# The sums of weight blocks in two squared-ReLU MLPs, moved from GpSimd to VectorE

## The chip, the core and the metric

The kernel runs on one core of a Trainium2 chip. The metric is the device time of one execution in microseconds. A core has a matrix engine (TensorE, "PE" in the profile, with its weight loads as "PEld"), VectorE ("DVE"), ScalarE ("ACT"), GpSimd ("POOL"), and SyncE ("SP"), which here only issues transfers. POOL issues transfers too, among them those that add to what lies in DRAM.

## The reference, cut to what matters

Two layers of a residual network over 1024 tokens of width 1024. Each layer mixes tokens (a recurrent block in layer 0, a forgetting attention in layer 1, each beside a memory cross-attention) and then applies an MLP of width 4096:

```python
def sqrelu_mlp(h, w1, w2):
    return jnp.square(jax.nn.relu(h @ w1)) @ w2

def reference(x, mem, ...):
    for layer in range(DEPTH):          # DEPTH = 2
        ...                             # token mixer, memory attention
        x = x + jnp.concatenate([y_mix, y_mem], axis=-1) @ w_out[layer]
        x = x + sqrelu_mlp(rms_norm(x, norm_mlp[layer]), w_mlp_in[layer], w_mlp_out[layer])
    return x
```

All tensors are float32.

## The kernel before, in words

**Precision.** TensorE multiplies in fp32r, a rounded form of float32. Every operand is therefore split into a high part, written by ScalarE as a rounding copy, and a low part, the operand less its high part, written by VectorE. A product then takes three matmuls: high times high, high times low, low times high (`t3`). For weights the two halves of a split are `_wpart`: the copy at line 316 (tile `wh`), the difference at line 317 (tile `wl`). For activations they are lines 474 and 477 (`split_sb`; both write a tile `r`) or 468 and 469 (`split`).

**Seven products in place of eight.** The MLPs use a scheme of Strassen's kind. Both factors are cut in two by two blocks, and seven products of block sums replace the eight block products. One *unit* (class `Unit`) is one two-by-two set of weight blocks a11, a12, a21, a22, each 128 x 1024, of which the seven left factors are formed: a11, a12, S2, S3, S1, a22 and S4, in this order. Each of the two MLPs runs over eight groups g, and each group over two units: a `w1` unit (`mlp_z`, the hidden layer) and a `w2` unit (`mlp_out`, the output layer). That makes 32 units, and seven products of 24 matmuls for each.

**Block sums.** `_wunit` makes a factor. For six of the seven it only splits a buffer. For S2 it also forms the sums, in place, in two halves of 512 columns: a11 - a21 (line 355, becomes S3), x = a22 - S3 (line 356, is S2 and lies in a float32 tile `f`), a12 - x (line 357, becomes S4); then over all 1024 columns a21 + a22 (line 360, becomes S1). So a unit has seven summing instructions: six of 128 x 512 and one of 128 x 1024. The engine is `G`: VectorE where `unit.dve` is true, GpSimd elsewhere. `plan_mlp` sets it for the `w1` unit of group 0 alone, once for each layer. The splits of S2, at line 317 from the tile `f`, are on ScalarE and VectorE in either case.

**Weights on their way.** Raw blocks come from DRAM by SP into four buffers `wr` (line 312). A buffer takes its next block when its last factor has been split. The split factors lie in a ring of three pairs `wh`, `wl`, so a factor is split at most two products ahead of the one that uses it (`wnext`, `_wsplit`).

**Activations.** `mlp_z` ends a hidden block by an addition from PSUM (line 1033), a rectification and scaling (line 1037), a square on ScalarE (line 1038) and block sums of its own (lines 1138, 1141, 1147, 1149), and then splits for the right factors of `mlp_out`. ScalarE copies first partial results out of PSUM at line 1028. In all groups but the last, `mlp_out` sends results by adding transfers from the POOL queue (line 1172, tile `xspill`), and a tile is free again when its transfer has landed. In the last group, GpSimd adds some results (line 1192) or fetches with adding transfers (line 1195). In layer 1 the first products of groups 0 to 3 are made earlier ("parked"), so the units of these groups hold fewer factors, but the sums are all there.

**Order.** The Python code emits instructions in program order. The tile framework, with `schedule_with_timeline_sim=True`, then fixes each engine's order at build time with a planner that plays the program through with costs of its own, and takes, of what is ready, what was emitted first. On the chip each engine works its own queue strictly in that order.

Of the kernel before, what the change touches and what calls it, by code (L numbers as in the profile page):

```python
# [175 lines left out]
class Builder:  # L176
# [825 lines left out]
    def plan_mlp(self, l, parked, wait):  # L1002
        for g in wait:
            self.plan_unit("w1", 8 * l + g, Unit.ALL[1:2])
        for g in range(8):
            u = self.plan_unit("w1", 8 * l + g, Unit.ALL[2:] if g in parked + wait else Unit.ALL)
            u.dve = g == 0
            self.plan_unit("w2", 8 * l + g)

    def product(self, banks, parts, start, done=None):  # L1010
        w = self.wnext()
# [779 lines left out]
```

## Time and profile before

| | |
|---|---|
| runs of the kernel before | 2135.48, 2134.29, 2131.20 us; median 2134.29 us |
| the profiled execution | 2132.37 us, span 2130.7 us |
| PE busy | 2071.5 us, 97% of the span |
| DVE busy | 1663.3 us, 78% |
| ACT busy | 1141.9 us, 54% |
| POOL busy | 864.0 us, 41% |
| adding transfers on POOL (line 1172) | 224, 284.7 us busy |
| mean granted TensorE clock | 0.988 of full speed |

The first MLP takes the stretch from some 340 to 980 us, the second from some 1505 us to the end, with a few of its first products a little earlier. A row of the groups reads: line, engine, operation, output <- input, shapes, count, then busy time in us and the mean of one in ns, then the time that the engine stood idle just before them and what ended it. A row of the timeline reads: start and length in us, engine, line, operation, and in brackets the idle time before it with the engine, tile and line that ended it.

### The profile page before, as it was taken

How to read it: one execution, taken by the hardware profiler on the slowest of the kernel's cores; microseconds unless marked ns; L12 is line 12 of the kernel's file. 1: busy time of each engine (PE TensorE's matmuls, PEld its weight loads, DVE VectorE, ACT ScalarE, POOL GpSimd, SP SyncE). 2: the span in 40 equal slices, each digit the busy share in tenths (PEclk: the TensorE clock that was granted, in tenths of full speed). 3: DMA queues.
4: the chain of work that ended last, by engine and by line, in shares of the span. 5: the costliest groups of instructions: out<-in, count | busy, mean ns of one | idle time of the engine just before them, and what ended most of it. 6: DMA issues, size and time to landing. Idle time of an engine off the chain costs nothing. (4 is left out here: it accounts for less than half of the span.)

```text
span 2130.7 us, 30055 instructions
## 1 busy us (share of the span) xinstructions
PE 2071.5 (97%) x10466; PEld 1727.4 (81%) x10466; DVE 1663.3 (78%) x2708; ACT 1141.9 (54%) x2160; POOL 864.0 (41%) x844
## 2 busy tenths in 40 slices
PE   9999999999999999988999999999999999999998
PEld 8898878878778778767998998777777877787786
DVE  7988698877877877887677778776787768868777
ACT  6755655544454454555555646566544554445443
POOL 2222321535535525545342333422054645445444
PEclk8999999999999999989999999999999999999999
DMA  5422452546545635627768446934546675364474
GB/s 180 140 77 93 135 184 94 101 89 128 101 97 119 111 87 119 156 86 199 276 218 290 133 138 214 299 122 129 161 99 139 138 150 101 85 140 94 89 173 119
DMA packets 126392, 298.44 MB, mean 140 GB/s; under 512 B 14176, under 2 KB 16288, under 8 KB 126240
## 3 DMA queue, kind: packets, MB, share of 16 engines
q1 hardware_dynamic: 82464, 208.36, 29.4%
q0 software_dynamic: 43776, 88.17, 23.2%
q8 instruction: 82, 1.34, 0.3%
q14 instruction: 70, 0.57, 0.1%
HBM read 187.32 MB, written 109.15 MB: 139 GB/s over the span
## 5 line engine op out<-in xcount | busy, mean ns | idle before, releaser
L317 DVE TENSOR_TENSOR wl<-wr,wh 128x1024 fp32r<-128x1024 f32 (+2 forms) x362 | 441.2, 1229 | 108.5 <-ACT wh L316 104.1
L1017 PE MATMUL pspt<-r,wh 128*128 128x512 f32 x1536 | 485.1, 396 | 7.2 <-DVE r L477 2.6
L1172 POOL DMA_DIRECT2D xspill<-f x224 | 284.7, 1963 | 287.5 <-DVE f L1033 284.1
L316 ACT ACTIVATE wh<-wr 128x1024 fp32r<-128x1024 f32 (+3 forms) x411 | 306.0, 766 | 141.4 <-PE pss L1017 41.2
L1017 PEld LDWEIGHTS pspt<-r,wh 128*128 128x128 f32 x1536 | 289.0, 188 | 77.9 <-DVE r L477 4.3
L1017 PE MATMUL pss<-r,wh 128*128 128x512 f32 x1024 | 329.6, 400 | 19.8 <-ACT f L1028 8.1
L477 DVE TENSOR_TENSOR r<-f,r 128x512 fp32r<-128x512 f32 x282 | 230.1, 826 | 98.5 <-ACT r L474 39.9
L1017 PE MATMUL pspt<-r,wl 128*128 128x512 f32 x768 | 305.6, 398 | 0.2
L1017 PE MATMUL pspj<-r,wh 128*128 128x512 f32 x832 | 265.8, 399 | 2.1 <-DVE f L1033 1.0
L1017 PEld LDWEIGHTS pss<-r,wh 128*128 128x128 f32 x1024 | 192.6, 189 | 75.9 <-DVE r L477 13.9
L385 PE MATMUL pspj<-wh,r 128*128 128x256 f32 (+1 forms) x1280 | 248.5, 286 | 2.3 <-DVE r L1322 0.8
L474 ACT ACTIVATE r<-f 128x512 fp32r<-128x512 f32 x282 | 173.5, 626 | 106.2 <-DMA xspill<-f 49.0
L1038 ACT ACTIVATE f<-f 128x512 f32<-128x512 f32 x128 | 80.9, 632 | 269.5 <-DVE f L1037 269.4
L385 PEld LDWEIGHTS pspj<-wh,r 128*128 128x128 f32 x1280 | 201.6, 188 | 5.3 <-DVE r L1322 1.0
L1017 PE MATMUL pss<-r,wl 128*128 128x512 f32 x512 | 203.6, 398 | 0.0
L355 POOL TENSOR_TENSOR wr<-wr,wr 128x512 f32<-128x512 f32 x60 | 95.7, 1778 | 249.0 <-DVE wl L317 233.2
L1017 PEld LDWEIGHTS pspj<-r,wh 128*128 128x128 f32 x832 | 156.3, 189 | 39.4 <-DVE r L469 1.5
L385 PE MATMUL pspj<-wl,r 128*128 128x256 f32 (+1 forms) x640 | 181.1, 283 | 0.0
L1017 PEld LDWEIGHTS pspt<-r,wl 128*128 128x128 f32 x768 | 146.0, 190 | 36.9 <-DVE wl L317 2.0
L385 PE MATMUL pspj<-r,wh 128*128 128x512 f32 x488 | 164.1, 411 | 5.3 <-ACT r L474 2.1
L1017 PE MATMUL pspj<-r,wl 128*128 128x512 f32 x416 | 163.4, 397 | 0.6 <-DVE wl L317 0.5
L357 POOL TENSOR_TENSOR wr<-wr,f 128x512 f32<-128x512 f32 x60 | 135.4, 2550 | 17.1 <-issue 17.1
(301 smaller groups left out, 4035.3 us busy)
## 6 DMA issues: line engine op xcount, KB each, us to landing
wr<-in_w_dram SPq DMA_DIRECT2D x136, 512.0 KB, 4.5
xspill<-f POOLq DMA_DIRECT2D x224, 256.0 KB, 7.0
f<-xspill SPq DMA_DIRECT2D x88, 256.0 KB, 4.1
xspill<-f SPq DMA_DIRECT2D x64, 256.0 KB, 3.5
f<-in_xT_dram SPq DMA_DIRECT2D x32, 256.0 KB, 3.5
wr<-in_wkv_dram SPq DMA_DIRECT2D x16, 512.0 KB, 3.6
wr<-in_wina_dram SPq DMA_DIRECT2D x15, 512.0 KB, 3.6
wsp<-wh SPq DMA_DIRECT2D x14, 512.0 KB, 5.4
```

The costliest lines, as they stand in the source:

```text
L316: self.wact = self.nc.scalar.activation(hi, raw, AF.Copy)
L317: eng.tensor_tensor(lo, raw, hi.bitcast(F32), ALU.subtract)
L355: G.tensor_tensor(r["a11"][:, d], r["a11"][:, d], r["a21"][:, d], ALU.subtract)
L357: G.tensor_tensor(r["a12"][:, d], r["a12"][:, d], x, ALU.subtract)
L385: self.lastmm = self.nc.tensor.matmul(out, lhsT=a, rhs=b, start=(j == 0), stop=(j == n - 1))
L474: i = self.nc.scalar.activation(hi[:, :n], src, AF.Copy)
L477: self.nc.vector.tensor_tensor(lo[:, :n], src, hi[:, :n].bitcast(F32), ALU.subtract)
L1017: self.lastmm = self.nc.tensor.matmul(ps, lhsT=a, rhs=b, start=(start and c == 0 and j == 0), stop=(c == n - 1 and j == 2), skip_group_che ...
L1038: self.lastsq = self.nc.scalar.activation(f[:, n], f[:, n], AF.Square)
L1172: nc.gpsimd.dma_start(self.xs[2 * q + a, :, b * H:(b + 1) * H], f[:, n], accum_op=ALU.add)
```

## The change

The flag `dve` is set for every unit in `plan_mlp`, so that `G` is VectorE in all 32 units. Nothing else differs in the source: the same instructions with the same operands in the same program order, 30 units' sums under another engine. What follows from it in the build is that the planner makes all queues anew.

```diff
         for g in range(8):
             u = self.plan_unit("w1", 8 * l + g, Unit.ALL[2:] if g in parked + wait else Unit.ALL)
-            u.dve = g == 0
-            self.plan_unit("w2", 8 * l + g)
+            u.dve = True
+            self.plan_unit("w2", 8 * l + g).dve = True
```

Units of layer 1's parked products, planned elsewhere with `Unit.ALL[:2]`, `[:1]` and `[1:2]`, have no S2 and so no sums.

## The prediction

> **What bounds the kernel now.** I read the page's first part, then busy time by stretch, then the waits of the matrix engine, then the timeline where they lie.
>
> ```profile
> span 2130.7 us, 30055 instructions
> PE 2071.5 (97%) x10466; PEld 1727.4 (81%) x10466; DVE 1663.3 (78%) x2708; ACT 1141.9 (54%) x2160; POOL 864.0 (41%) x844
> ```
>
> ```profile
> 500.00:600.00 100.00, 99.63 (x428) 79.86 (x427) 73.86 (x76) 48.09 (x76) 46.54 (x38) 1.00 0.57 115
> ...
> 930.00:940.00 10.00, 8.88 (x39) 6.91 (x38) 10.00 (x11) 9.05 (x20) 7.92 (x7) 1.00 0.00 0
> 940.00:950.00 10.00, 5.22 (x16) 3.35 (x15) 10.00 (x11) 3.77 (x6) 5.87 (x4) 0.72 0.00 0
> ...
> 1560.00:1575.00 15.00, 11.11 (x37) 8.58 (x36) 12.93 (x14) 5.86 (x10) 8.13 (x7) 0.77 0.52 107
> 2090.00:2105.00 15.00, 11.36 (x40) 8.06 (x40) 15.00 (x18) 8.34 (x14) 6.45 (x4) 0.89 0.06 23
> ```
>
> Columns: stretch, length, busy PE, PEld, DVE, ACT, POOL, then granted clock. TensorE bounds the MLPs: within them it is busy 99.63 of 100 us, and no faster vector work can make that shorter. What can be had is its few stalls: short ones once in each group, longer ones where an MLP's first or last group runs. In the last groups (930 to 950, 2090 to 2105) DVE is busy without a break, 10.00 of 10 and 15.00 of 15 us: there DVE is late, and there its work is the price.
>
> But part of that DVE time is no work. Groups of the steady stretch 400 to 900 us, 13 units:
>
> ```profile
> L317 DVE TENSOR_TENSOR wl<-wr,wh 128x1024 fp32r<-128x1024 f32 x77 | 149.8, 1945 | 34.4 <-ACT wh L316 32.7 <-issue 1.6
> L477 DVE TENSOR_TENSOR r<-f,r 128x512 fp32r<-128x512 f32 x86 | 68.1, 803 | 46.4 <-DMA xspill<-f 22.9 <-ACT r L474 17.9 <-ACT f L1028 5.6
> L317 DVE TENSOR_TENSOR wl<-f,wh 128x512 fp32r<-128x512 f32 x26 | 44.1, 1717 | 9.1 <-ACT wh L316 9.1
> L1037 DVE SCALAR_TENSOR_TENSOR f<-f,f 128x512 f32<-128x512 f32 x36 | 33.3, 926 | 0.8
> ...
> L357 POOL TENSOR_TENSOR wr<-wr,f 128x512 f32<-128x512 f32 x26 | 63.9, 2792 | 7.3 <-issue 7.3
> L356 POOL TENSOR_TENSOR f<-wr,wr 128x512 f32<-128x512 f32 x26 | 57.9, 2696 | 0.0
> L360 POOL TENSOR_TENSOR wr<-wr,wr 128x1024 f32<-128x1024 f32 x13 | 48.1, 3701 | 0.0
> L355 POOL TENSOR_TENSOR wr<-wr,wr 128x512 f32<-128x512 f32 x26 | 42.0, 1869 | 107.2 <-DVE wl L317 107.2
> ```
>
> The two units whose sums are on DVE already give the lone price of these shapes (minimum, median, maximum in ns):
>
> ```profile
> L355 DVE TENSOR_TENSOR wr<-wr,wr x4: 680/682/692, 332.5 to 1441.7; 128x512 f32<-128x512 f32 x4
> L360 DVE TENSOR_TENSOR wr<-wr,wr x2: 1207/1212/1218, 338.6 to 1513.2; 128x1024 f32<-128x1024 f32 x2
> ```
>
> So a DVE instruction with two operands in SBUF takes 0.68 us for 512 columns and 1.21 for 1024, but 1.72 and 1.95 on average where POOL forms sums. One took 9.76:
>
> ```profile
> 413.28 9.76 DVE L317 TENSOR_TENSOR wl<-wr,wh 128x1024 fp32r<-128x1024 f32 x1
> ```
>
> **The change, part by part.**
>
> *Added to DVE.* Six instructions of 0.68 and one of 1.21 make 5.3 us for a unit, 158 us for 30.
>
> *Removed from DVE.* In the stretch above, against the lone times: 77 x (1.945 - 1.21) = 56.6; 26 x (1.717 - 0.68) = 27.0; 86 x (0.803 - 0.68) = 10.6; 36 x (0.926 - 0.68) = 8.9. That is 103 us for 13 units, 7.9 for one, 238 for 30. That all of it goes with the sums I conclude from where it lies (below). Net, DVE loses some 80 us of its 1663. Its total does not bound the time, so this alone gives nothing.
>
> *What it does on the path.* One steady group, where TensorE waits once, in the third product of `mlp_out`:
>
> ```profile
> 609.39 1.31 DVE L477 TENSOR_TENSOR r<-f,r 128x512 fp32r<-128x512 f32 x1
> 610.63 1.78 DVE L1037 SCALAR_TENSOR_TENSOR f<-f,f 128x512 f32<-128x512 f32 x1
> 612.33 3.43 DVE L317 TENSOR_TENSOR wl<-wr,wh 128x1024 fp32r<-128x1024 f32 x1
> ...
> 616.29 1.46 DVE L317 TENSOR_TENSOR wl<-f,wh 128x512 fp32r<-128x512 f32 x1
> 617.67 1.78 DVE L477 TENSOR_TENSOR r<-f,r 128x512 fp32r<-128x512 f32 x1
> ...
> 628.33 0.68 DVE L477 TENSOR_TENSOR r<-f,r 128x512 fp32r<-128x512 f32 x1
> ```
>
> ```profile
> 605.90 3.00 POOL L355 TENSOR_TENSOR wr<-wr,wr 128x512 f32<-128x512 f32 x2 [16.92 <-DVE wl L317]
> ```
>
> ```profile
> 627.95 0.87 PE L1017 MATMUL pspj<-r,wh 128*128 128x512 f32 x3
> 629.06 0.50 PE L1017 MATMUL pss<-r,wh 128*128 128x512 f32 x1 [0.24 <-DVE r L477]
> ```
>
> Three matmuls at 0.233 us (428 in 99.63, window row above) from 627.95 put the next one at 628.65; it came at 629.06, 0.41 late, when the split at 628.33 had ended. DVE worked without a break from 609.39 until then. Five instructions are stretched, all between 609 and 620, while POOL's sums run; over their lone times they lose 0.63 + 1.10 + 2.22 + 0.78 + 1.10 = 5.8 us. In their place come at most 5.3 us of sums. So even if the planner puts all seven ahead of that split, it comes 0.5 us earlier, and the 0.41 goes. If it leaves the three that aren't needed so soon (lines 357 and 360, 2.6 us) for later, 3.1 us earlier. Late next is ScalarE's high part of the same split, whose work also shifts, because it waits for DVE. The waits of the whole run:
>
> ```profile
> PE pss L1017 <- DVE r L477: 7.2, 13, 3.1
> ...
> ACT wh L316 <- POOL f L356: 61.1, 30, 4.1
> ```
>
> ```profile
> PE pss L1017 <- DVE r L477: 1.7, 2, 1.3
> ```
>
> ```profile
> 739.27 0.50 PE L1017 MATMUL pspj<-r,wl 128*128 128x512 f32 x1 [0.52 <-DVE wl L317]
> ```
>
> Of the first row's 13 stalls the longest, 3.1 us, is in the last group of layer 1, and two of 1.7 us together lie between 930 and 985, the last group of layer 0 (third row, the waits of that stretch alone). That leaves ten with 2.4 us, 0.24 each as above: ten steady stalls that each cost 0.41. With 0.5 us for a weight split that came late behind another long instruction (739.27) they make 4.6 us, all gained. The second row, ScalarE standing 30 times before POOL's x, shrinks to DVE's speed; I price it at nothing, since TensorE is covered by two products of split weights ahead, 11 us.
>
> *The last group of layer 1.* The same stretch, now with a stall of 3.06 us:
>
> ```profile
> 2074.29 1.41 DVE L477 TENSOR_TENSOR r<-f,r 128x512 fp32r<-128x512 f32 x1
> ...
> 2085.80 1.77 DVE L477 TENSOR_TENSOR r<-f,r 128x512 fp32r<-128x512 f32 x1
> ```
>
> ```profile
> 2096.30 0.50 PE L1017 MATMUL pss<-r,wh 128*128 128x512 f32 x1 [3.06 <-DVE r L477]
> ```
>
> Seven instructions from the first to the last of these rows are stretched, by 7.1 us together; 5.3 come in. Gain 1.8; the ends are 0 and 3.1, the whole stall.
>
> *The last group of layer 0.* DVE is full (window rows above); POOL's later additions for the memory keys stay and go on stretching. Removed as in the steady group 5.8, added 5.3: I take 1.0, since some sums can come after the stretch; ends -2 (a worse order) and 5.8 (all sums later).
>
> *First groups of layer 1.* I take 1.0 together for groups 1 and 2, whose stall waits for sends that start when DVE's additions end, 0.5 us earlier in each; nothing for group 0; ends 0 and 4.
>
> *POOL's queue.* With the sums gone, sends no longer stand behind them. The steady stall above hangs on no send, so I price this at nothing; ends 0 and 2 us of gain, as tiles come free sooner.
>
> *Queues that the sums join.* DVE is now behind raw loads of a21 and a22, and behind a waiting sum stands all else of DVE. In steady groups POOL's first sum is released by the split of a11, not by a load (16.92 above; 107.2 of 107.2 in the groups), so there is nothing to wait for; the exception is the third rival.
>
> *Sum.* 4.6 + 1.8 + 1.0 + 1.0 = 8.4 us. The profiled execution took 2132.4 us (1.7 around its span), so it would take 2124.0. It lies 1.9 us under the median of 2134.3; against the median I forecast 2126.
>
> A rule on the clock stands beside this. The clock was 0.89 from 2090 to 2105, around the stall of 3.06. From 940 to 950 it was 0.72, where the longest wait was shorter:
>
> ```profile
> 943.10 0.50 PE L1017 MATMUL pspt<-r,wh 128*128 128x512 f32 x1 [2.58 <-DVE r L477]
> ```
>
> The Trainium skill ("TensorE: Matmul & The Clock Gate", "Why this matters for your kernels") says to keep idle gaps of TensorE under about 3 us, or its clock halves; by that rule the stall cut to 1.3 us would also keep its clock, 15 x 0.11 = 1.7 us more, and the sum would be 10.1. The trace only half agrees: the clock fell beside waits of 2.58 us and less too. I leave it out of the sum.
>
> **The rivals.**
>
> *No change that can be measured.* The planner puts all sums ahead of the awaited splits and DVE's stretches stay nearly as long (5.3 for 5.8); ScalarE is late next and keeps half of each 0.41. Gain 2 us: 2132. For it: the two numbers are near each other. Against it: three of the seven sums are not needed soon.
>
> *Larger gain.* The planner defers sums, and all 5.8 to 7.1 us come off the full stretches: 4.6 steady, 5.8 and 3.1 in the last groups, 4 in the first ones, and 2 for earlier sends: 19.5 us, 2115. For it: 4.78 us of stall in 940 to 950, 3.89 in 1560 to 1575. Against: their waits hang on ScalarE and sends too.
>
> *Slower: DVE stands before late raw loads.* The place is the first groups of layer 1.
>
> ```profile
> 1651.27 3.87 POOL L355 TENSOR_TENSOR wr<-wr,wr 128x512 f32<-128x512 f32 x2 [7.27 <-DMA wr<-in_w_dram]
> 1657.63 2.54 POOL L356 TENSOR_TENSOR f<-wr,wr 128x512 f32<-128x512 f32 x2 [2.49 <-DMA wr<-in_w_dram]
> ...
> 1720.77 2.99 POOL L355 TENSOR_TENSOR wr<-wr,wr 128x512 f32<-128x512 f32 x2 [6.97 <-DMA wr<-in_w_dram]
> ```
>
> ```profile
> 1649.82 0.73 PE L1017 MATMUL pss<-r,wh 128*128 128x512 f32 x2 [1.45 <-ACT f L1028]
> ```
>
> Here loads ended POOL's waits, 16.7 us in these three, and TensorE has no cover, as its stall shows. If the planner expects the loads sooner than they come, DVE stands those 16.7 us with splits and evacuations behind it: 2134.3 - 8.4 + 16.7 = 2143. It decides from 8.4 us of such waits on. Against it: the sums are emitted after the work then due, so in the planner's order they only go ahead of it if they look ready.
>
> *Sends starved.* 224 sends remain on POOL.
>
> ```profile
> 627.63 0.87 POOL L1172 DMA_DIRECT2D xspill<-f  x1 [8.73 <-DVE f L1033]
> ```
>
> If dense DVE work held back a send by one DVE instruction, 0.7 us, tiles would come free later by that in the two groups that wait for them, and not elsewhere: 1.4 us, so 2127; with the ten steady stalls kept as well, 2131. This send ran 0.87 us while DVE was busy without a break, so I give it little. The Trainium skill ("SBUF — State Buffer", "SBUF: two separate sides") warns of this: VectorE in a two-port mode keeps GpSimd from writing descriptors. The row shows no such delay beside these two-operand instructions.
>
> **How the numbers follow.** Forecast (2118 to 2130) 0.46; larger gain 0.10; no change 0.20; sends starved 0.03; slower by late loads, or by an unlucky new order of that size, 0.21. About 0.2%, 4.3 us, is what a measurement of this kernel can tell from no change. Faster is 0.56, same 0.23, slower 0.21. The range reaches from somewhat below the larger gain, 2109, to just above the third rival, 2144; the forecast's own is 2118 to 2130.
>
> **What would show it.** Lines 355 to 360 on DVE at 0.68 and 1.21 us; line 317 of 1024 columns back from 1.95 to near 1.22 in 400 to 900; DVE busy near 1585; sends at 0.87 us; TensorE's waits for line 477 down from 13 to a few. I am wrong if DVE's idle time before lines 355 and 356 ends with loads, if line 317 stays near 1.9, or if the splits at the third product come later than now.

## The result, and the profile after

The changed kernel takes 2118.76 us (median; 2118.58 to 2119.57) against 2132.74 us (2130.55 to 2135.48) for the kernel before on the same chip: a ratio of 0.9931, 95% interval 0.9915 to 0.9947. It is 14 us faster; the forecast was 8.4. The profiled execution took 2119.57 us.

The page of the changed kernel, first part:

```profile
span 2117.8 us, 29975 instructions
PE 2065.7 (98%) x10466; PEld 1733.3 (82%) x10466; DVE 1594.5 (75%) x2918; ACT 1154.8 (55%) x2160; POOL 513.8 (24%) x634
```

DVE has 210 instructions more and 69 us less to do. Its groups in the steady stretch 400 to 900 us:

```profile
L317 DVE TENSOR_TENSOR wl<-wr,wh 128x1024 fp32r<-128x1024 f32 x76 | 93.1, 1225 | 79.4 <-ACT wh L316 78.8
L477 DVE TENSOR_TENSOR r<-f,r 128x512 fp32r<-128x512 f32 x87 | 58.7, 694 | 35.0 <-DMA xspill<-f 23.1 <-ACT r L474 7.3 <-ACT f L1028 4.5
...
L1037 DVE SCALAR_TENSOR_TENSOR f<-f,f 128x512 f32<-128x512 f32 x37 | 25.5, 689 | 0.7
L317 DVE TENSOR_TENSOR wl<-f,wh 128x512 fp32r<-128x512 f32 x26 | 17.9, 690 | 2.2 <-ACT wh L316 2.2
```

All four are at their lone price: 1.95, 0.80, 0.93 and 1.72 us have become 1.23, 0.69, 0.69 and 0.69. The same steady group as in the prediction, DVE's timeline:

```profile
605.62 0.69 DVE L1033 TENSOR_TENSOR f<-f,pss 128x512 f32<-128x512 f32 x1 [0.18 <-PE pss L1017]
606.22 1.29 DVE L355 TENSOR_TENSOR wr<-wr,wr 128x512 f32<-128x512 f32 x2
607.43 0.69 DVE L1037 SCALAR_TENSOR_TENSOR f<-f,f 128x512 f32<-128x512 f32 x1
608.03 1.29 DVE L356 TENSOR_TENSOR f<-wr,wr 128x512 f32<-128x512 f32 x2
609.23 1.22 DVE L360 TENSOR_TENSOR wr<-wr,wr 128x1024 f32<-128x1024 f32 x1
...
614.50 1.30 DVE L357 TENSOR_TENSOR wr<-wr,f 128x512 f32<-128x512 f32 x2
...
626.46 0.70 DVE L477 TENSOR_TENSOR r<-f,r 128x512 fp32r<-128x512 f32 x1
```

All seven sums are done by 615.80, ahead of the split at 626.46 (last row). No wait is left here, as the row for 500 to 600 us shows (columns as in the prediction): TensorE is busy 100.00 of 100 us, where it was 99.63.

```profile
500.00:600.00 100.00, 100.00 (x431) 80.91 (x430) 64.38 (x88) 48.31 (x74) 14.03 (x17) 1.00 0.51 111
```

Of what TensorE still waits for in the whole run, the two largest rows:

```profile
PE pspt L1017 <- DVE r L477: 7.8, 1, 7.8
PE pss L1017 <- DVE r L477: 6.7, 2, 3.3
```

The 13 waits of the second row's kind are now two, and a single long one (first row) has come in the last group of layer 0, where several of up to 2.6 us stood before. Where the time came from can be read by matching the 5376 matmuls of line 1017 one by one and taking the start of each in the changed kernel less its start before. The second column is the profile of the result, the third a second profile of the same kernel:

| stretch | result | again | predicted gain |
|---|---|---|---|
| up to the first MLP | +1.4 | +1.7 | - |
| layer 0, groups 0 to 6 | -4.8 | -4.7 | 4.6 with layer 1's |
| layer 0, last group, up to layer 1's MLP | -2.4 | -0.9 | 1.0 |
| layer 1, up to the start of group 1 | +1.1 | +0.9 | 0 |
| layer 1, groups 1 and 2 | -6.4 | -6.6 | 1.0 |
| layer 1, groups 3 to 6 | -2.8 | -2.8 | in the 4.6 |
| layer 1, last group | +0.3 | -1.0 | 1.8 |

### The profile page after: what moved, and what is told of

Same layout as the page of the kernel before. It is cut to its first block, busy times and chain, and to the rows that moved or that the text cites. A ratio compares the mean times of both kernels' runs of the same rounds, so it can differ in the third digit from the quotient of the medians.

```text
span 2117.8 us, 29975 instructions
## 1 busy us (share of the span) xinstructions
PE 2065.7 (98%) x10466; PEld 1733.3 (82%) x10466; DVE 1594.5 (75%) x2918; ACT 1154.8 (55%) x2160; POOL 513.8 (24%) x634
## 5 line engine op out<-in xcount | busy, mean ns | idle before, releaser
L1017 PE MATMUL pspt<-r,wh 128*128 128x512 f32 x1536 | 492.3, 396 | 12.1 <-DVE r L477 7.8
L317 DVE TENSOR_TENSOR wl<-wr,wh 128x1024 fp32r<-128x1024 f32 (+2 forms) x362 | 352.2, 984 | 191.6 <-ACT wh L316 190.4
L1172 POOL DMA_DIRECT2D xspill<-f x224 | 196.0, 1091 | 831.5 <-DVE f L1033 802.7
L1017 PE MATMUL pspj<-r,wh 128*128 128x512 f32 x832 | 271.4, 399 | 2.1 <-DVE f L1033 1.0
L477 DVE TENSOR_TENSOR r<-f,r 128x512 fp32r<-128x512 f32 x282 | 193.1, 702 | 75.2 <-DMA xspill<-f 45.0
L385 PE MATMUL pspj<-r,wh 128*128 128x512 f32 x488 | 164.3, 411 | 5.4 <-ACT r L474 2.1
L385 PEld LDWEIGHTS pspj<-wl,r 128*128 128x128 f32 x640 | 120.5, 188 | 1.0 <-issue 0.2
L1017 PEld LDWEIGHTS pss<-r,wl 128*128 128x128 f32 x512 | 97.7, 191 | 23.8 <-issue 0.2
```

The lines of the kernel that those rows point to most:

```text
L317: eng.tensor_tensor(lo, raw, hi.bitcast(F32), ALU.subtract)
L385: self.lastmm = self.nc.tensor.matmul(out, lhsT=a, rhs=b, start=(j == 0), stop=(j == n - 1))
L477: self.nc.vector.tensor_tensor(lo[:, :n], src, hi[:, :n].bitcast(F32), ALU.subtract)
L1017: self.lastmm = self.nc.tensor.matmul(ps, lhsT=a, rhs=b, start=(start and c == 0 and j == 0), stop=(c == n - 1 and j == 2), skip_group_che ...
L1172: nc.gpsimd.dma_start(self.xs[2 * q + a, :, b * H:(b + 1) * H], f[:, n], accum_op=ALU.add)
```

## The experiments

In each, the kernel before or the changed one was taken and a few lines altered; times are medians, and each is compared with runs of the kernel before on its own chip.

### Half of the units

The first has the second unit of each group (`mlp_out`'s) on VectorE, the first unit as before.

```diff
-            u.dve = True
+            u.dve = g == 0
```

> Sums on VectorE for the 16 w2 units (and for the two w1 units of group 0, as before), on GpSimd for the other 14 w1 units. Theory (a GpSimd sum stretches VectorE's two-operand instructions, and only the stretch that ends at the third product of mlp_out costs TensorE time; that stretch runs beside the w2 sums): nearly the whole gain, 2119 to 2123 us, no steady stall of 0.41 left, line 317 of 1024 columns still at 2.5 us and more beside the w1 sums. Rival 'sends' (the gain is that adding transfers no longer stand behind sums in GpSimd's queue; it is the w1 sums that lie among the sends): no gain, 2130 to 2135 us. Rival 'order' (a luckier plan of all queues): anything, with no relation to the units.

2122.90 us, ratio 0.9947 (0.9932 to 0.9962): 12 us gained.

```diff
-            self.plan_unit("w2", 8 * l + g).dve = True
+            self.plan_unit("w2", 8 * l + g)
```

> The complement: sums on VectorE for the 16 w1 units, on GpSimd for the 16 w2 units. Theory: the stretched instructions before the third product of mlp_out stay and so do the steady stalls; only the two late weight splits go: 2129 to 2134 us. Rival 'sends': the whole gain, 2117 to 2123 us. If both halves add up, the two gains sum to about 14 us.

2133.72 us, ratio 0.9999 (0.9987 to 1.001): nothing. Groups of 400 to 900, of the first of these kernels and then of the second:

```profile
L317 DVE TENSOR_TENSOR wl<-wr,wh 128x1024 fp32r<-128x1024 f32 x77 | 127.6, 1657 | 65.4 <-ACT wh L316 64.7
L477 DVE TENSOR_TENSOR r<-f,r 128x512 fp32r<-128x512 f32 x87 | 58.0, 683 | 33.0 <-DMA xspill<-f 16.2 <-ACT r L474 6.8 <-ACT wh L316 6.1
```

```profile
L317 DVE TENSOR_TENSOR wl<-wr,wh 128x1024 fp32r<-128x1024 f32 x77 | 107.1, 1391 | 61.1 <-ACT wh L316 59.5 <-issue 1.6
L477 DVE TENSOR_TENSOR r<-f,r 128x512 fp32r<-128x512 f32 x86 | 67.9, 801 | 45.4 <-DMA xspill<-f 18.1 <-ACT r L474 16.2 <-ACT f L1028 5.6
L1037 DVE SCALAR_TENSOR_TENSOR f<-f,f 128x512 f32<-128x512 f32 x36 | 33.3, 925 | 0.8
```

The kernel that gains nothing took more off line 317: 149.8 us came down to 107.1 there, and only to 127.6 in the kernel that gains 12 us. But it left the activations' lines 477 and 1037 as they were (0.80 and 0.93 before), and with them TensorE's wait, as its own row shows:

```profile
PE pss L1017 <- DVE r L477: 6.9, 14, 3.1
```

So the gain does not follow how much of the stretching goes, but which instructions it held: the second units' sums run beside those for which the third product of `mlp_out` waits, and what the first units' sums stretch has cover. The sends, ahead of which no sum of the first units stands any more in the second kernel, take 196.8 us of GpSimd's time there in place of 284.7, and that brings nothing: their rival fails.

### GpSimd writes, or reads, and forms no sum

Two kernels from the one before, in which GpSimd's sums are replaced; VectorE gets none. First, three constant writes for each sum:

```diff
-            G.tensor_tensor(r["a11"][:, d], r["a11"][:, d], r["a21"][:, d], ALU.subtract)
+            for _ in range(3):
+                nc.gpsimd.memset(r["a11"][:, d], 0.5)
...
```

> The kernel before, in which GpSimd's 210 summing instructions of 30 units are replaced by writes of a constant to the same tiles, three for each, so that GpSimd is occupied about as long at the same places but reads nothing from SBUF; VectorE gets no sums. The sums are left out of the computation. Theory (what stretches VectorE is GpSimd reading its two operands): line 317 of 1024 columns falls to 1.2 us, the steady stalls go, 2112 to 2120 us. Rival 'sums sooner' (the gain of the change is that VectorE has the sums ready in 5 us in place of 16): 2126 to 2133 us, as GpSimd is as slow as before. Rival 'sends': 2128 to 2133 us, as the sends still stand behind as much work.

2101.49 us, ratio 0.9843 (0.9825 to 0.9861): below every range that I had written down, the theory's 2112 to 2120 too; why is told further down. Second, one addition of a block to itself for each sum:

```diff
-            G.tensor_tensor(r["a11"][:, d], r["a11"][:, d], r["a21"][:, d], ALU.subtract)
+            G.tensor_tensor(r["a11"][:, d], r["a11"][:, d], r["a11"][:, d], ALU.add)
...
```

> The kernel before, with each of GpSimd's sums replaced by an addition of the same shape of one block to itself (a11 + a11 twice, a12 + a12, a21 + a21), so that no block sum is formed there and the output is another. Beside the kernel with constant writes in the same places (2101.49 us, line 317 at 1.22 us) this differs in one thing: GpSimd reads, two operands from SBUF, as its sums do. Theory: the reads are what stretches VectorE, so everything of the kernel before comes back: line 317 of 1024 columns at 1.8 to 2.1 us from 400 to 900, 2126 to 2136 us. Rival: it was the wait for the sums, or for the loads and blocks that they join (x from a22, S1 from a22), or GpSimd's time as such, that cost: 2101 to 2108 us, line 317 at 1.2 to 1.3.

2108.01 us, ratio 0.9861 (0.9844 to 0.9877). DVE's groups of 400 to 900 in the kernel with writes, where line 489 is line 477 of the other kernels:

```profile
L317 DVE TENSOR_TENSOR wl<-wr,wh 128x1024 fp32r<-128x1024 f32 x78 | 95.2, 1221 | 79.9 <-ACT wh L316 79.3
L489 DVE TENSOR_TENSOR r<-f,r 128x512 fp32r<-128x512 f32 x86 | 57.8, 684 | 39.0 <-DMA xspill<-f 22.7 <-ACT f L1040 5.8 <-ACT wh L316 5.4
...
L317 DVE TENSOR_TENSOR wl<-f,wh 128x512 fp32r<-128x512 f32 x26 | 17.9, 688 | 22.7 <-ACT wh L316 22.7
```

and in the kernel with self-additions, where line 485 is line 477:

```profile
L317 DVE TENSOR_TENSOR wl<-wr,wh 128x1024 fp32r<-128x1024 f32 x77 | 96.7, 1255 | 69.3 <-ACT wh L316 69.3
L485 DVE TENSOR_TENSOR r<-f,r 128x512 fp32r<-128x512 f32 x86 | 78.8, 927 | 43.3 <-DMA xspill<-f 28.0 <-ACT r L482 10.0 <-ACT wh L316 5.2
L317 DVE TENSOR_TENSOR wl<-f,wh 128x512 fp32r<-128x512 f32 x26 | 34.2, 1324 | 13.3 <-ACT wh L316 13.0
L1041 DVE TENSOR_TENSOR f<-f,pspt 128x512 f32<-128x512 f32 x51 | 33.6, 677 | 12.5 <-PE pspt L1025 12.5
```

GpSimd is busy 858.5 and 797.6 us in the two, near the 864.0 before; from 400 to 900 us what stands in place of the sums takes 211 and 156 us of it, and the sums before took 212. With writes nothing on VectorE is stretched; with reads the two-operand forms are, and the one that reads PSUM (0.677) is not. The Trainium skill ("SBUF — State Buffer", "Who interferes with whom") says just this: a VectorE instruction with two inputs in SBUF contends with a GpSimd instruction that reads SBUF, and not with one that only writes it. Both traces agree.

My size for the second kernel was wrong, though. I expected all the stretching back; what came back in this stretch is 77 x 0.045 + 86 x 0.247 + 26 x 0.644 = 41 us for 13 units, 3.2 for one, of 7.9. At 3.2 us a unit the ten steady stalls stay away: by the matched matmuls the groups 0 to 6 of layer 0 gain 4.7 us over the kernel before, as much as in the changed kernel. So both figures of the rival came out, 2108.01 us at the edge of its range and line 317 at 1.26. What parts the two theories is the stretch of VectorE's queue before the third product of `mlp_out`, in the group of the prediction:

```profile
610.88 1.58 DVE L485 TENSOR_TENSOR r<-f,r 128x512 fp32r<-128x512 f32 x1
...
614.72 1.14 DVE L317 TENSOR_TENSOR wl<-f,wh 128x512 fp32r<-128x512 f32 x1
615.79 1.52 DVE L485 TENSOR_TENSOR r<-f,r 128x512 fp32r<-128x512 f32 x1
...
626.19 0.68 DVE L485 TENSOR_TENSOR r<-f,r 128x512 fp32r<-128x512 f32 x1
```

These three lose 2.2 us over the lone price, where five lost 5.8 before, and the awaited split (last row) comes 3.6 us sooner after the same addition from PSUM (at 608.79 us before, 610.27 here); 0.41 was needed. In groups 1 to 6 of layer 0, VectorE's instructions from the last product of `mlp_z` to that third product lose some 5.7 us over their lone price in each group of the kernel before and of the one with the first units' sums moved, the two that have the stall. They lose 2.1 to 2.3 with self-additions, and nothing with writes, with the second units' sums moved and in the changed kernel, the four that have none. In the kernel before VectorE does not stand idle once from 609.39 us to the awaited split, so no wait for a sum or a block explains that it came late. Why a block added to itself does less harm than two blocks is open: its instructions are shorter too (1.60 against 1.87 us at the first sum), and its a21 + a21 runs at another time than a21 + a22 did.

### GpSimd repeats every sum

The changed kernel, with GpSimd reading the blocks again after VectorE's sums and writing to a tile that nothing uses.

```diff
+            for c in (0, 256):
+                e = slice(h * 512 + c, h * 512 + c + 256)
+                P_.tensor_tensor(self.scr, r["a11"][:, e], r["a21"][:, e], ALU.subtract)
...
```

> The changed kernel, and beside it GpSimd forms every sum a second time, in pieces of 256 columns into a scratch tile that nothing reads. Theory: the stretching comes back and VectorE has the sums as well, so the awaited splits come some 5 us later in each group than before the change: 2145 to 2200 us. Rivals 'sums sooner' and 'order': VectorE's own sums are as soon as in the changed kernel, 2118 to 2124 us. Rival 'sends': 2128 to 2135 us.

2239.62 us, ratio 1.0491 (1.0473 to 1.051), 121 us more than the changed kernel, and far more than I expected. The waits of VectorE say why this can't be read as the price of the reads:

```profile
DVE wr L368 <- POOL scr L363: 73.8, 22, 5.5
```

Line 368 is a21 + a22, in place: it had to wait until GpSimd had read the old a21. The repeats put a new wait on VectorE's queue, with everything behind it. The run mixes the price of a wait for GpSimd in VectorE's queue with that of the reads (the weight splits of 1024 columns take 1.32 us here); as a test of the theory it is inconclusive.

### Where in the run

Four kernels on one chip, with the changed kernel again as their base.

> The changed kernel once more, as the base for the runs beside it. Both theories: 2117 to 2121 us, 13 to 15 us under the kernel before.

2116.72 us, ratio 0.9922 (0.9909 to 0.9936). Then the sums on VectorE in groups 1 and 2 of layer 1 alone:

```diff
-            u.dve = True
-            self.plan_unit("w2", 8 * l + g).dve = True
+            u.dve = g == 0 or l == 1 and g in (1, 2)
+            self.plan_unit("w2", 8 * l + g).dve = l == 1 and g in (1, 2)
```

> Sums on VectorE only in the two units of groups 1 and 2 of layer 1 (and, as before, in the first unit of each layer). Theory 1: the 6.4 us that the changed kernel gains between the starts of groups 1 and 3 come from these four units alone, because VectorE's stretched instructions there hold back the sends and splits for which TensorE waits: 5 to 7 us under the kernel before, 2127 to 2129 with the base at 2134, the stalls of 1.6 and 2.96 us gone. Rival A: the gain there needs the head start that the earlier groups give (sends, tiles and loads that run ahead): 0 to 3 us under. Rival B, the size of the forecast's term: 1 us under.

2126.98 us, ratio 0.9966 (0.9952 to 0.9979): 6.2 us gained by four units of 30 (3.7 by the two profiled spans, with 1.9 lost ahead of group 1). By the matched matmuls 6.4 us come in from the start of group 1 on, and 5.2 of them are left where group 3 starts. The term is local, and it is five to six times what I had put there. The reverse, the last groups' sums back on GpSimd:

```diff
-            u.dve = True
-            self.plan_unit("w2", 8 * l + g).dve = True
+            u.dve = g < 7
+            self.plan_unit("w2", 8 * l + g).dve = g < 7
```

> All sums on VectorE but those of the four units of the two last groups, which GpSimd forms as before. The forecast's terms for the last groups, 1.0 and 1.8 us: 2.8 us slower than the changed kernel, about 2122. Theory from the two traces (layer 1's last group gives nothing, layer 0's up to 2.4 with what follows it): 0 to 2.4 us slower. Rival: the last groups are where VectorE is full, so the sums harm there and GpSimd is the better place: 1 to 4 us faster than the changed kernel.

2120.53 us, ratio 0.9937 (0.9924 to 0.9951): by the medians 3.8 us slower than the changed kernel, by the two spans 1.7. GpSimd is not the better place there. Nor is the forecast's 2.8 for the two last groups borne out: by the matched matmuls only 0.6 of the 1.7 us lies in them, and 1.3 lie in group 4 of layer 1, whose sums are on VectorE in both kernels.

### What is left in the last groups

GpSimd still adds there. The changed kernel's timelines, DVE and POOL, in the last group of layer 0, and DVE's in that of layer 1:

```profile
931.62 8.64 DVE L590 SCALAR_TENSOR_TENSOR r<-f,par,r 128x256 fp32r<-128x256 f32 x6
```

```profile
931.09 4.67 POOL L597 TENSOR_TENSOR f<-f,f 128x512 f32<-128x512 f32 x3 [36.75 <-ACT f L593]
935.72 5.67 POOL L1192 TENSOR_TENSOR f<-f,f 128x512 f32<-128x512 f32 x4
```

```profile
2072.19 1.78 DVE L1138 TENSOR_TENSOR f<-f,f 128x512 f32<-128x512 f32 x1
2073.89 1.78 DVE L477 TENSOR_TENSOR r<-f,r 128x512 fp32r<-128x512 f32 x1
```

So I gave VectorE these additions too:

```diff
-                nc.gpsimd.tensor_tensor(ss[:, :H], ss[:, :H], sq[:, :H], ALU.add)
+                (nc.vector if l else nc.gpsimd).tensor_tensor(ss[:, :H], ss[:, :H], sq[:, :H], ALU.add)
...
-                    G.tensor_tensor(dst[q][:, n], dst[q][:, n], f[:, n], ALU.add)
+                    V.tensor_tensor(dst[q][:, n], dst[q][:, n], f[:, n], ALU.add)
```

> The changed kernel with two more kinds of additions moved from GpSimd to VectorE: those of line 1192 in the last groups, and those of line 597 for the memory keys of layer 1, which run beside the last group of layer 0. Theory: what GpSimd still reads there stretches VectorE (one normalising pass at line 590 took 8.64 us beside three such additions, and lines 1138 and 477 1.77 beside line 1192), so moving them gives 3 to 6 us: 2113 to 2117. Rival: VectorE is full there with work of its own, and the additions only lengthen it: 0 to 4 us slower. Rival 2: those stretches hang on ScalarE and the adding transfers: within 1 us of the changed kernel.

2111.88 us, ratio 0.9901 (0.9888 to 0.9915), beside the changed kernel's 2116.72 on the same chip. In this kernel's DVE timeline the passes of line 590 are short again (four of them in 1.67, where six took 8.64), with the additions among them:

```profile
930.19 1.67 DVE L590 SCALAR_TENSOR_TENSOR r<-f,par,r 128x256 fp32r<-128x256 f32 x4
931.78 0.69 DVE L597 TENSOR_TENSOR f<-f,f 128x512 f32<-128x512 f32 x1
```

By the matched matmuls it gains 4.7 us over the changed kernel at the last group of layer 0 and 3.4 at that of layer 1 (6.2 and 2.0 over the changed kernel's second profile), and gives 1.7 to 2.0 back in layer 1 ahead of group 1; another 1.5 to 1.8 come in ahead of the first MLP, unexplained. The same mechanism, in two places that the change had not touched. One step further, the squares that GpSimd forms in the last group of layer 0:

```diff
-                self.sqacc(1 if b in seen else 0, b, x, V if b == 0 and a == 1 else None)
+                self.sqacc(1 if b in seen else 0, b, x, V)
```

> The kernel with lines 1192 and 597 on VectorE, and besides them the squares and their additions that GpSimd does in the last group of layer 0 for the sums over the rows. Theory: no reading instruction of GpSimd is left beside that group, VectorE's stretched passes there all come down, 1 to 4 us gained, 2108 to 2111 with the base at 2133. Rival: VectorE is full there by its own work, and 16 more instructions of about 0.7 us cost 3 to 11 us, 2115 to 2123.

2110.79 us, ratio 0.9878 (0.9858 to 0.9899), the fastest kernel here that computes the reference; ten instructions went over, not 16. Against the one before it, the interval cannot tell a gain from none. Last, the kernel before that with one unit given back:

```diff
-            self.plan_unit("w2", 8 * l + g).dve = True
+            self.plan_unit("w2", 8 * l + g).dve = (l, g) != (1, 0)
```

> The kernel with lines 1192 and 597 on VectorE (1.0099 times faster than before in its own run, 21 us), and the sums of one unit given back to GpSimd: the second unit of group 0 of layer 1, where the changed kernel lost 1.1 us and VectorE is full. Theory: 1 to 3 us gained, so 2109 to 2111 with the base at 2133. Rival: GpSimd's reads stretch VectorE by 7.9 us for the 5.3 us of sums that it saves, so 0 to 3 us lost: 2112 to 2115.

2116.22 us, ratio 0.9911 (0.9894 to 0.9928). It gained nothing. Of the 6.5 us by which its matched matmuls end later than without that unit's return, 4.0 are there before the second MLP begins, so the 2 to 4 us that the rival names are not shown either.

### What the sums cost VectorE

The kernel with constant writes took 17 us less than the changed one. The sums that VectorE now forms must be the price, but where?

```diff
+            if unit.dve:
...
+            else:
+                self._wpart(hi[:, d], lo[:, d], r["a22"][:, d], V)
...
+            u.dve = g < 7 and (l, g) != (1, 0)
...
```

> The changed kernel with the block sums of six units left out on every engine: both units of the two last groups and of group 0 of layer 1 (S2 is then split straight from a22, S3, S1 and S4 from the raw blocks; all splits and all matmuls stay, so the output is another). Theory: only in these groups is VectorE full, so there the sums of 5.3 us for a unit are paid in full by TensorE, while elsewhere they are free: what leaving out every GpSimd sum gained beyond the changed kernel, some 16 us, comes from these six units: 12 to 17 us under the changed kernel, about 2102 to 2106. Rival: the sums are hidden there too, and that further gain came from an order that happened to be better, or from many groups: within 4 us of the changed kernel.

2102.29 us, ratio 0.9846 (0.9826 to 0.9866): leaving out six units' sums of 32 gains 14 to 16 us over the changed kernel's two medians. The matched matmuls place 8.9 us of it in layer 1 ahead of group 1 and 6.3 in layer 1's last group; layer 0's last group gives 0.3 (8.6, 4.9 and 1.8 against the changed kernel's second profile). The row for 1500 to 1560 us, of the changed kernel and then of this one:

```profile
1500.00:1560.00 60.00, 56.24 (x254) 44.37 (x253) 53.13 (x87) 36.38 (x58) 1.41 (x4) 1.00 0.27 86
```

```profile
1500.00:1560.00 60.00, 60.00 (x278) 49.08 (x278) 51.05 (x84) 37.45 (x60) 4.16 (x7) 1.00 0.32 99
```

TensorE stands 3.8 us there with the sums and not at all without. The kernel with constant writes, which leaves all of GpSimd's sums out, is no quicker than the changed kernel in the groups in between: within 0.1 us from group 0 to 6 of layer 0 and from group 1 to 6 of layer 1. So there the sums on VectorE are free, and at the edges those of six units, 28.5 us of VectorE's busy time (1594.5 less 1566.0), cost some 15.

## Why the prediction was right, and where its sizes were off

**The mechanism held.** Sums run at the lone price on VectorE and its other two-operand instructions come back to theirs. DVE fell by 69 us to 1594.5, where I had 80 and 1585. Both terms behind that were too large: with constant writes, where VectorE gets no sums, its busy time is 1464.3, so some 199 us of stretching went, not 238, and the sums then add some 130, not 158. In the last groups the remaining additions of GpSimd still stretch it.

**The steady stalls, 4.6 forecast, 7.6 found.** The count of ten was exact: six in layer 0 and four in layer 1, each at `pss` of the third product, and all are gone. The size was short, because a late matmul makes the next one late as well. The kernel before again:

```profile
629.06 0.50 PE L1017 MATMUL pss<-r,wh 128*128 128x512 f32 x1 [0.24 <-DVE r L477]
629.40 0.40 PE L1017 MATMUL pss<-r,wl 128*128 128x512 f32 x1
```

0.34 us lie between these two starts, 0.10 over the usual 0.233. So each stall cost 0.51, and ten make 5.1; the rest are late weight splits that cost up to 0.8 each, of which I had counted one, at 0.5. I had also left open whether the planner would put the sums behind the awaited split. It put all seven ahead, my worse case, and no stall came, also because the first two fill time in which VectorE had waited, as in the kernel before here:

```profile
608.79 0.69 DVE L1033 TENSOR_TENSOR f<-f,pss 128x512 f32<-128x512 f32 x1 [1.05 <-PE pss L1017]
```

**Groups 1 and 2 of layer 1, 1.0 forecast, 6.4 found.** This is the step that was mis-sized: I let the sends start 0.5 us earlier. The kernel before, from an addition that both kernels make straight after the same product to the last one that releases sends in group 1, and the stall of group 2:

```profile
1617.06 0.69 DVE L1033 TENSOR_TENSOR f<-f,pss 128x512 f32<-128x512 f32 x1 [0.18 <-PE pss L1017]
...
1619.86 0.69 DVE L1033 TENSOR_TENSOR f<-f,pss 128x512 f32<-128x512 f32 x1 [1.05 <-PE pss L1017]
...
1641.80 0.67 DVE L1033 TENSOR_TENSOR f<-f,pso 128x512 f32<-128x512 f32 x1
```

```profile
1720.96 0.73 PE L1017 MATMUL pss<-r,wh 128*128 128x512 f32 x2 [2.80 <-ACT f L1028]
```

The same in the changed kernel:

```profile
1612.35 0.69 DVE L1033 TENSOR_TENSOR f<-f,pss 128x512 f32<-128x512 f32 x1 [0.18 <-PE pss L1017]
1612.96 1.29 DVE L355 TENSOR_TENSOR wr<-wr,wr 128x512 f32<-128x512 f32 x2
...
1633.79 0.70 DVE L1033 TENSOR_TENSOR f<-f,pso 128x512 f32<-128x512 f32 x1
```

From first start to last end VectorE takes 25.4 us before and 22.1 after, so the sends are released 3.3 us earlier, not 0.5. The sums from 1612.96 on fill the 1.05 us that VectorE had waited there. In the changed kernel the stalls of group 1 (1.45 in the prediction's row) and of group 2 (2.80) are both gone whole. I had charged all 5.3 us of sums to that stretch and nothing to its idle time, and took the stall for the wait that would shrink by just as much as the sends move; my upper end of 4 was too low with it. That most of the 6.4 us belongs to these four units is shown by their own run, which keeps 5.2; how they divide between idle time, the order and the second stall is worked out from these rows, not tested.

**Last group of layer 1, 1.8 forecast, between -0.3 and 1.0 found; of layer 0, 1.0 forecast, 0.9 to 2.4.** I subtracted added from removed as if all the stretching went. It stays in part, by line 1192; with those additions moved too, layer 1's group gains 2.0 to 3.4 us more. The rule of the Trainium skill that I weighed there ("TensorE: Matmul & The Clock Gate", "Why this matters for your kernels", gaps under about 3 us) needed the stall to shrink to 1.3, and it did not. By the starts of the matmuls it was 3.2 us before, 3.5 in both profiles of the changed kernel, and 2.2 in both kernels with the additions moved. The clock from 2065 to 2110 us, in this order, the one with the squares moved last:

```profile
2065.00:2110.00 45.00, 41.65 (x168) 33.23 (x167) 31.41 (x42) 18.17 (x30) 14.02 (x12) 0.92 0.38 87
2065.00:2110.00 45.00, 41.65 (x174) 33.35 (x173) 34.17 (x45) 19.04 (x32) 14.03 (x12) 0.96 0.41 97
```

```profile
2065.00:2110.00 45.00, 38.40 (x162) 30.02 (x160) 29.68 (x45) 16.45 (x27) 7.24 (x8) 0.98 0.52 141
2065.00:2110.00 45.00, 37.34 (x151) 29.05 (x149) 27.07 (x41) 14.08 (x23) 7.22 (x8) 0.94 0.52 140
```

The same stall goes with 0.92 and 0.96, and the shorter one with 0.98 and 0.94. So these runs do not bear out that a stall under 3 us keeps the clock, and neither does the 0.72 beside waits of 2.58 us and less in the prediction's rows; leaving the rule out of the sum was right.

**Group 0 of layer 1, nothing forecast, 1.1 lost.** Here VectorE is busy 53.13 of 60 us (row for 1500 to 1560 us above), and the run with six units' sums left out shows them paid for.

**The rivals.** The time lies 7.2 us under my number, only 0.8 inside the range that I gave the forecast, and 3.8 over the larger gain's 2115, but that rival's condition, sums deferred, did not hold. That it fell inside is in part luck: what groups 1 and 2 of layer 1 gave beyond my 1.0 was partly offset by losses that I had not forecast, ahead of the first MLP and in group 0. Late raw loads are there and small: VectorE's waits for them in layer 1, in the changed kernel, make 3.4 us. Of these 2.9 lie between 1640 and 1730 us, where TensorE waits for nothing.

```profile
DVE f L356 <- DMA wr<-in_w_dram: 2.5, 3, 1.1
DVE wr L357 <- DMA wr<-in_w_dram: 0.9, 2, 0.7
```

Sends were not starved: the mean of one is 1.09 us (row below) where it was 1.96 beside the sums, and the median 0.88 where it was 1.60.

```profile
L1172 POOL DMA_DIRECT2D xspill<-f x224 | 196.0, 1091 | 831.5 <-DVE f L1033 802.7 <-ACT f L1028 26.8 <-issue 1.5
```

The 1.4 to 1.7 us lost ahead of the first MLP are unexplained; the kernels here differ by up to 3.3 us at that point.

## What to carry to other kernels

Before moving work off an engine because it is slow there, look at what it does to its neighbour: here GpSimd's sums made VectorE lose more time than it now spends on forming them. Price such a move by the instructions that a product waits for, not by the total: one half of the units gave 12 us, and the other half, which took more off the weight splits, nothing. And let added work fill idle time first; where the engine has none, as in group 0 of layer 1 and in its last group, the added work is paid for.

## What the hardware showed that I had not expected

A late matmul costs more than its wait: the next one starts 0.10 us late too, in each of the ten steady stalls. GpSimd's writes of constants, 211 us of busy time from 400 to 900 us, left VectorE's instructions at 1.22 and 0.68 to 0.69 us, while additions of a block to itself brought line 477 to 0.93 but line 317 only to 1.26, so the stretching depends on more than the number of operands that GpSimd reads; on what, is open.
